# Source order for every engine and the transfer queue in the last stages of a hybrid decoder layer, with the attention cut into six phases

## The chip, the cores and the metric

The kernel runs on one core of a Trainium2 chip. The metric is the device time of one execution in microseconds (us). The engines are TensorE (PE in the rows), VectorE (DVE), ScalarE (ACT), GpSimd (POOL) and SyncE (SP), which issues nearly all transfers; each works through its own list of instructions in order and waits for semaphores of the others.

## What is computed

One decoder layer for 512 tokens of width 1024. The normalised input goes through one projection of 3,380 columns, cut into three mixers: gated linear attention (4 heads, chunks of 64), sparse attention (6 heads of 64; an indexer's scores pick the 128 keys of each query) and a causal pooling mixer (4 groups with windows 2, 4, 8, 16). Each is multiplied by a SiLU gate; one output projection, a residual and a final norm follow. Cut to the core:

```python
h = rmsnorm(x, norm_g[l])
p = jnp.einsum('btd,dc->btc', h, w_in[l])
(gq, gk, gv, gz, ggate, dq, dk, dv, dgate, qi, ki, wi, pu, pgate) = split_cols(p)
glog = log_sigmoid(einsum('btr,rc->btc', gz, gla_gate_w2[l]) + gla_gate_b[l]) / 16
y_gla = rmsnorm(gla_mixer(gq, gk, gv, glog), gla_norm_g[l]) * silu(ggate)
# dsa: score = sum over index heads of relu(qi.ki) * wi, causal; top 128 keys of a query;
#      softmax over them of q.k / 8 + bias[bucket(distance)]; times v
y_dsa = dsa_mixer(dq, dk, dv, qi, ki, wi, rel_bias) * silu(dgate)
y_pool = pool_mixer(pu, pool_w[l], pool_scale[l]) * silu(pgate)
x = x + einsum('btc,cd->btd', concat([y_gla, y_dsa, y_pool]), w_out[l])
return rmsnorm(x, final_norm_g)
```

## The kernel before

**Products.** Matmuls are done in parts: a weight or an operand is split into a high part (`hi_of`, ScalarE) and a low part (`lo_of`, VectorE, or POOL for the weight halves named in `POOL_LO`), and a product is three matmuls, high by high, high by low and low by high. A weight chunk (`qd`, `n1` to `n4`, `dg`, `pg`, `c2`, `c1`, `pu`, `c0`) comes in two halves through a few staging buffers; `halves("c11")` splits half 1 of chunk `c1`. The output weights `wo0` to `wo3` come through the same buffers in two loads each, and four pairs of `oh`, `ol` pieces are split from each.

**Order.** `open_run` starts the layer. Then `project` goes through the chunks; each chunk has steps (projections into one accumulator), and after half a step ("mid") or a whole one `hooks` runs what the table `after` names for that place. So the table puts the other work between the projections: index scores, the top-128 rounds (`topk(i, ...)`: one MAX8 and one MATCH_REPLACE8 over the query tile's row of 256, 384 or 512 columns take eight keys; 16 rounds each for tiles 1, 2, 3), the linear attention (`gla_...`), and from chunk `pu` on the sparse attention. Inside `manual_schedule` an engine's list is the order of the source for the engines named; others are filled by a scheduler. Up to chunk `c1` that names TensorE, ScalarE, VectorE and POOL; from the first attention item on, and in `finish`, only TensorE and POOL. SyncE's list is the scheduler's after the opening.

**Attention.** An item (i, g) is query tile i (128 queries) and head pair g. `att_l` makes bias and mask in L on POOL; `att_q` makes the scores (TensorE, ps from KK, KL and QQ), adds them to L and takes the row's extremum (VectorE, L694), the exponential (ScalarE, L696), the reciprocal (VectorE, L698) and the normalised L (POOL, L700); `att_t` transposes L (tpp) and copies it to pt (ScalarE for one head, VectorE for the other); `att_v` makes ov and yt, and their parts yDh and yDl. KK, KL and QQ hold keys and queries of a head pair; `take_dqk` makes them from a projection (qkr), its high part qkh and its low part qkl, which are put in place by transfers. Chunk `c1` brings the queries of pair 2 in its first step and keys in its second; the first scores, item (0,2), stand right behind it.

**Linear attention.** `gla_gates` multiplies GS by w2r (split in high and low at that place) to z, then `gtA` (ScalarE) and `gtM` (VectorE); `gla_sums` subtracts and scans; `gla_scores` makes AT with masked copies; `gla_out` (po) needs AT. `pool_branch` is four scans and small operations on VectorE. `finish` holds the output projection (op), the rest of the attention and the norm.

Of the kernel before, what the change touches and what calls it, by code (L numbers as in the profile page):

```python
# [29 lines left out]
POOL_LO = ("n11", "n21", "n31", "n41", "pg0", "c20", "c21", "c10", "pu0")  # L30
# [39 lines left out]
def hybrid_layer(  # L70
# [102 lines left out]
    def bias_load():  # L173
        with tc.issue_after(chunks[-1].load.ins):
            nc.sync.dma_start(TB, bias_tab.rearrange("p (h j) -> p h j", h=6))
# [182 lines left out]
    def take_dqk(c, j):  # L358
        for step, cc in enumerate((0, 1) if j == 1 else (1, 0)):
# [31 lines left out]
    def gla_gates():  # L391
# [5 lines left out]
        hi_of(w2r, w2s)  # L397
        lo_of(w2r[32:48], w2s[32:48], w2r[32:48])
# [176 lines left out]
    def pool_branch():  # L575
        pm = S("pm", [P, 2, T])
        for j in range(2):
            for b, w in ((0, (2, 8)[j]), (64, (4, 16)[j])):
                r = slice(b, b + 64)
                nc.vector.tensor_tensor_scan(pm[r, j, :], up[r, j, 16:528], up[r, j, 16 - w:528 - w], 0.0,  # L580
                                             op0=ALU.add, op1=ALU.subtract)
            pf = S("pf", [P, 16], bufs=2, name=f"pf{j}")
            nc.vector.tensor_tensor(pf, pm[:, j, 0:16], rcn[:, j, :], op=ALU.mult)
            nc.vector.scalar_tensor_tensor(pm[:, j, :], pm[:, j, :], rcw[:, j:j + 1], up[:, j, 16:528],
                                           op0=ALU.mult, op1=ALU.subtract)
            nc.vector.tensor_tensor(pm[:, j, 0:16], pf, up[:, j, 16:32], op=ALU.subtract)
# [24 lines left out]
    halves = lambda *names: [partial(half, n[:2], int(n[2])) for n in names]  # L611
    after = {
# [465 lines left out]
```

## Time and profile before

| | us |
|---|---|
| median of 3 runs (lowest to highest) | 281.83 (281.48 to 282.24) |
| the profiled execution, and its span | 280.79, 279.0 |
| TensorE busy (share of the span), instructions | 251.5 (90%), 1498 |
| VectorE | 203.4 (73%), 444 |
| ScalarE | 120.7 (43%), 251 |
| POOL | 95.3 (34%), 107 |
| mean granted clock of TensorE | 0.959 |

The profile's page gives the busy time of every engine over the span, and a strip of 40 slices. In the strip TensorE has eights and nines nearly everywhere, with one slice at 5 about three fifths through; the granted clock falls to 5 and 7 there. The waits and the timeline then tell what stood in the way, and the windows give busy time and clock of any stretch. A busy share is an average over stages: what counts for the end is which engine's next instruction is late.

### The profile page before, as it was taken

How to read it: one execution, taken by the hardware profiler on the slowest of the kernel's cores; microseconds unless marked ns; L12 is line 12 of the kernel's file. 1: busy time of each engine (PE TensorE's matmuls, PEld its weight loads, DVE VectorE, ACT ScalarE, POOL GpSimd, SP SyncE). 2: the span in 40 equal slices, each digit the busy share in tenths (PEclk: the TensorE clock that was granted, in tenths of full speed). 3: DMA queues.
4: the chain of work that ended last, by engine and by line, in shares of the span. 5: the costliest groups of instructions: out<-in, count | busy, mean ns of one | idle time of the engine just before them, and what ended most of it. 6: DMA issues, size and time to landing. Idle time of an engine off the chain costs nothing.

```text
span 279.0 us, 4219 instructions
## 1 busy us (share of the span) xinstructions
PE 251.5 (90%) x1498; PEld 210.6 (76%) x1498; DVE 203.4 (73%) x444; ACT 120.7 (43%) x251; POOL 95.3 (34%) x107
## 2 busy tenths in 40 slices
PE   8999999689999899999999519987995999999991
PEld 5788979589999798888888408765883677787890
DVE  3969688958999859896969788889597565345222
ACT  5737386574734263363123243333474354232111
POOL 1633464413093086135303005631244455100010
PEclk9999999979999999999999957999799899999998
DMA  7796402225213220315246832840383000023221
GB/s 256 275 318 276 157 15 82 79 75 188 78 49 105 76 66 12 93 60 152 76 109 179 252 87 62 209 162 0 78 301 75 0 4 0 0 89 130 84 78 75
DMA packets 11780, 31.09 MB, mean 111 GB/s; under 512 B 1600, under 2 KB 1600, under 8 KB 11760
## 3 DMA queue, kind: packets, MB, share of 16 engines
q1 hardware_dynamic: 11328, 30.05, 34.6%
q10 hardware_dynamic: 432, 0.79, 0.8%
q8 instruction: 12, 0.20, 0.3%
q14 instruction: 8, 0.07, 0.1%
HBM read 23.91 MB, written 2.10 MB: 93 GB/s over the span
## 4 chain that ended last, share of the span: by engine, by line
PE 57%; DVE 25%; ACT 6%; issue 4%; DMA 4%; POOL 1%; POOLq 0%; DVEq 0%; ACTq 0%
PE op L749 13%; PE pf L915 8%; DVE scs L457 5%; PE pn_n L197 5%; DMA wr_wo<-in_w_out 4%; DVE m L456 4%; PE ov L720 3%; PE tpp L709 2%; DVE pm L580 2%; PE ps L692 2%; PE warm L936 2%; DVE wl_c L99 2%; ACT L L696 2%; DVE ol L99 2%; DVE wl_n L99 1%
## 5 line engine op out<-in xcount | busy, mean ns | idle before, releaser
L700 POOL TENSOR_SCALAR L<-L,ast 128x128 f32<-128x128 f32 (+3 forms) x24 | 12.7, 540 | 56.0 <-DVE ast L698 50.0
L456 DVE MAX8 m<-scs 128x8 f32<-128x256 f32 (+2 forms) x48 | 26.5, 553 | 0.2
L457 DVE MATCH_REPLACE8 scs<-m,scs 128x256 f32<-128x256 f32 (+2 forms) x48 | 26.1, 543 | 0.0
L197 PE MATMUL pn_n<-wh_n,hTh 128*128 128x270 f32 (+1 forms) x128 | 22.1, 296 | 0.0
L197 PE MATMUL pn_n<-wl_n,hTh 128*128 128x270 f32 (+1 forms) x128 | 21.8, 294 | 0.0
L197 PE MATMUL pn_n<-wh_n,hTl 128*128 128x270 f32 (+1 forms) x128 | 21.6, 292 | 0.0
L696 ACT ACTIVATE L<-L,ast 128x128 f32<-128x128 f32 (+3 forms) x24 | 13.3, 556 | 18.7 <-DVE ast L694 18.7
L209 PE MATMUL pt_c<-hTh,wh_c 128*128 128x512 f32 x48 | 19.7, 410 | 0.0
L197 PEld LDWEIGHTS pn_n<-wh_n,hTh 128*128 128x128 f32 x128 | 18.7, 193 | 0.7 <-issue 0.4
L210 PE MATMUL pt_c<-hTl,wh_c 128*128 128x512 f32 x48 | 19.1, 399 | 0.0
L211 PE MATMUL pt_c<-hTh,wl_c 128*128 128x512 f32 x48 | 19.1, 399 | 0.0
L197 PEld LDWEIGHTS pn_n<-wl_n,hTh 128*128 128x128 f32 x128 | 18.7, 197 | 0.0
L197 PEld LDWEIGHTS pn_n<-wh_n,hTl 128*128 128x128 f32 x128 | 18.4, 193 | 0.0
L692 PE MATMUL ps<-KK,QQ 128*128 128x128 f32 (+3 forms) x24 | 8.8, 373 | 10.1 <-DMA QQ<-qkl 9.1
L96 ACT ACTIVATE oh<-wr_wo 128x512 fp32r<-128x512 f32 x16 | 9.0, 622 | 18.4 <-DMA wr_wo<-in_w_out 13.6
L754 DVE TENSOR_TENSOR xr<-op,xr 128x512 f32<-128x512 f32 (+1 forms) x8 | 5.3, 657 | 15.7 <-PE op L749 15.7
L755 ACT ACTIVATE sqo<-xr 128x512 f32<-128x512 f32 (+1 forms) x8 | 4.8, 605 | 25.4 <-DVE xr L754 25.4
L99 DVE TENSOR_TENSOR ol<-wr_wo,oh 128x512 fp32r<-128x512 f32 x16 | 11.4, 744 | 5.1 <-ACT oh L96 5.0
L909 POOL TENSOR_TENSOR acc<-acc,sqk 128x512 f32<-128x512 f32 x7 | 9.5, 1354 | 15.1 <-ACT sqk L907 15.1
L99 POOL TENSOR_TENSOR wl_n<-wr_n,wh_n 128x1080 fp32r<-128x1080 f32 (+1 forms) x4 | 10.1, 2513 | 12.3 <-ACT wh_n L96 10.3
L692 PEld LDWEIGHTS ps<-KK,QQ 128*128 128x128 f32 x24 | 4.8, 201 | 11.6 <-DMA QQ<-qkl 9.5
L670 POOL TENSOR_TENSOR L<-scs,TB 128x512 f32<-128x512 f32 x9 | 12.6, 1403 | 0.0
(241 smaller groups left out, 718.4 us busy)
## 6 DMA issues: line engine op xcount, KB each, us to landing
wr_wo<-in_w_out SPq DMA_DIRECT2D x8, 512.0 KB, 3.7
wr_c<-in_w_in SPq DMA_DIRECT2D x6, 512.0 KB, 3.4
wr_n<-in_w_in SPq DMA_DIRECT2D x4, 540.0 KB, 7.9
wr_n<-in_w_in SPq DMA_DIRECT2D x4, 536.0 KB, 3.5
xr<-in_x SPq DMA_DIRECT2D x4, 512.0 KB, 4.1
xk<-in_x_t SPq DMA_DIRECT2D x7, 256.0 KB, 5.2
wk<-in_w_in SPq DMA_DIRECT2D x6, 256.0 KB, 5.0
KK<-qkh SPq DMA_DIRECT2D x12, 128.0 KB, 2.3
```

What stands on the lines that cost most here:

```text
L99: return (eng or nc.vector).tensor_tensor(dst, src, hi.bitcast(F32), op=ALU.subtract)
L197: mm(ps[:, 0:n], a[:, k, ts_], w[:, k, :], start=(h + part + k == 0), stop=(h == 1 and part == 2 and k == 3))
L209: mm(ps[:, t0:T], c.hi[h][:, k, cs], hTh[h][:, k, t0:T], start=(h + k == 0), stop=False)
L210: mm(ps[:, t0:T], c.hi[h][:, k, cs], hTl[h][:, k, t0:T], start=False, stop=False)
L211: mm(ps[:, t0:T], c.lo[h][:, k, cs], hTh[h][:, k, t0:T], start=False, stop=(h == 1 and k == 3))
L456: nc.vector.max(out=m8, in_=msk[i])
L457: nc.vector.match_replace(out=msk[i], in_to_replace=m8, in_values=msk[i], imm_value=TAKEN)
L692: mm(pss[b][:, 0:n], QQ[2 * g + b][:, i0:i0 + P], K[2 * g + b][:, 0:n], start=(K is KK), stop=(K is KL))
L696: nc.scalar.activation(L[:, b, 0:n], L[:, b, 0:n], AF.Exp, bias=st[:, b:b + 1], scale=-1.0, accum_out=st[:, 2 + b:3 + b])
L700: nc.gpsimd.tensor_scalar(L[:, b, 0:n], L[:, b, 0:n], st[:, 4 + b:5 + b], 1.0, op0=ALU.mult, op1=ALU.mult)
L749: mm(outs[t][a][:, 0:e - a], lhs, rhs, start=(first and yi == 0 and rhs is wh and lhs is yh), stop=(last and yi == len(ys) - 1 and lhs is yl))
L915: mm(pns[t], a[:, t * P:(t + 1) * P], w, start=(k + part == 0), stop=(k == KT - 1 and part == 2))
```

## The change

1. One `manual_schedule` block for all chunks and `finish`, naming TensorE, ScalarE, VectorE, POOL and SyncE: the source's order holds for all of them and for the transfers.
2. An attention item becomes six phases: l, q, n (reciprocal and normalise), t, v and y (the low part yDl), each with its place in `after` or `finish`. There is a new place, "end", behind a query or key step's transfers.
3. The split of w2r moves from `gla_gates` to `later_tables`; the logarithm becomes `gla_logs`, behind the split of `n30`; several weight splits move, and `c11` and `c00` get their low parts on POOL.
4. The top-128 rounds are set out so that all are placed by the end of the query step of `c1`; before, `topk(16, 2, 3)` put what remained behind `c1`.
5. The splits of the output weights (`split_out(n, h)`, two pieces each call) go to five places from `pu` on and into `finish`; before they stood together in `c0`. Their loads start while `c1` runs; `final_g` and the residual's x come in `finish`.
6. `pool_branch(j)` in two halves, `pool_low` and `out_norm` apart.

```diff
-POOL_LO = ("n11", "n21", "n31", "n41", "pg0", "c20", "c21", "c10", "pu0")
+POOL_LO = ("n11", "n21", "n31", "n41", "pg0", "c20", "c21", "c10", "c11", "pu0", "c00")
@@ later_tables
         nc.vector.tensor_copy(cm, of("cm"))
+        hi_of(w2r, w2s)
+        lo_of(w2r[32:48], w2s[32:48], w2r[32:48])
@@ take_dqk
                             nc.sync.dma_start(dst[2 * g + b][r:r + 64].bitcast(F32),
                                               src[64 * b:64 * b + 64].bitcast(F32))
+            hooks(c.name, step, "end")
@@ gla_gates
-        hi_of(w2r, w2s)
-        lo_of(w2r[32:48], w2s[32:48], w2r[32:48])
...
+
+    def gla_logs():
+        gtA = lt["gates"][0]
         nc.scalar.activation(gtA, gtA, AF.Ln, bias=1.0)
@@ after
-        ("n1", 3, "mid"): [partial(topk, 1, 2)],
-        ("n1", 3): [*halves("n30"), partial(topk, 1, 1, 3)],
+        ("n1", 3, "mid"): [*halves("n30"), lambda: gla_logs(), partial(topk, 1, 2)],
+        ("n1", 3): [partial(topk, 1, 1, 3)],
...
-        ("c1", 0): [late_tiles, *halves("pu1"), partial(topk, 2, 2, 3)],
-        ("c1", 1): [partial(topk, 16, 2, 3), *halves("c00", "c01")],
...
+        ("c1", 0, "mid"): [*halves("pu1"), partial(topk, 1, 2, 3)],
+        ("c1", 0, "end"): [*halves("c00"), partial(topk, 1, 2, 3)],
+        ("c1", 1, "mid"): [partial(topk, 1, 2, 3)],
+        ("c1", 1): [lambda: nc.gpsimd.memset(up[:, :, 0:16], 0.0), *att("l02", "l12")],
+        ("c1", 1, "end"): [*halves("c01"), partial(topk, 16, 2, 3), *att("q02")],
+        ("pu", 0, "mid"): att("n02", "q12"),
...
+        ("pu", 1, "mid"): [*att("v02", "t12", "q22"), lambda: pool_branch(0)],
+        ("pu", 1): [*att("y02", "n22"), lambda: split_out(0, 0), *att("v12", "l32")],
+        ("c0", 0, "mid"): [*att("y12", "t22", "q32"), lambda: pool_branch(1)],
+        ("c0", 0): att("n32", "l01"),
+        ("c0", 0, "end"): [lambda: split_out(1, 0), lambda: load_next(), *att("v22")],
+        ("c0", 1, "mid"): att("y22", "t32", "q01", "l11"),
...
+        ("c0", 1, "end"): [*att("v32", "q11", "l21"), lambda: split_out(0, 1)],
@@ att_q, att_n: the reciprocal and the normalising become a phase of their own
+    def att_n(i, g):
+
+        n = (i + 1) * P
+        L, st = Ls[i, g], asts[i, g]
         nc.vector.reciprocal(st[:, 4:6], st[:, 2:4])
@@ finish
-        att_t(0, 1), att_q(2, 1)
+        do("y32", "t01", "n11", "q21", "l00")
+        split_out(1, 1)
         out_part(1, 0, T, "G", first=True)
-        att_v(0, 1), att_t(1, 1), att_q(0, 0)
+        do("v01", "t11", "n21", "q00", "l31")
+        split_out(2, 0)
+        load_next()
...
         pool_mix()
         out_part(2, 0, T, "G", first=True)
-        att_v(1, 1), att_t(2, 1), att_q(3, 1)
+        do("y01")
+        pool_low()
+        do("v11", "t21", "n00", "q31", "l10")
+        split_out(3, 0)
         out_part(0, 0, T, "P")
...
+        do("y21", "v00", "t31", "n10", "q20", "l30")
+        split_out(3, 1)
+        do("y00")
         out_part(2, 0, T, "P")
         out_part(0, 0, T, "D", last=True)
@@ the end of the kernel
-    with tc.manual_schedule(engines={ENG.PE, ENG.Activation, ENG.DVE, ENG.Pool}):
-        project(("qd", "n1", "n2", "n3", "n4", "dg", "pg", "c2", "c1"))
-    with tc.manual_schedule(engines={ENG.PE, ENG.Pool}):
-        att_q(0, 2)
-        project(("pu", "c0"))
+    with tc.manual_schedule(engines={ENG.PE, ENG.Activation, ENG.DVE, ENG.Pool, ENG.SP}):
+        project([name for name, _ in CHUNKS])
         finish()
```

What an engine's list holds in a row, at three places. First SyncE's transfers around the end of chunk `c1` (QQ_110 and QQ_111 are the queries of pair 2, KK and KL keys, wr_wo output weights in their staging buffers), before:

```order
L381 DMA KK_115<-qkh_1642 64x512 x2
L147 DMA wr_wo_1667<-in_w_out 128x1024
L375 DMA QQ_110<-qkh_1695 64x512
L375 DMA QQ_111<-qkh_1695 64x512
L381 DMA KL_120<-qkl_1643 64x512 x2
L147 DMA wr_wo_1801<-in_w_out 128x1024
L381 DMA KL_121<-qkl_1643 64x512 x2
L375 DMA QQ_110<-qkl_1696 64x512
L375 DMA QQ_111<-qkl_1696 64x512
L381 DMA KK_112<-qkh_1749 64x512 x2
```

and after:

```order
L382 DMA KK_115<-qkh_1668 64x512 x2
L382 DMA KL_120<-qkl_1669 64x512 x2
L382 DMA KL_121<-qkl_1669 64x512 x2
L147 DMA wr_wo_1686<-in_w_out 128x1024
L147 DMA wr_wo_1688<-in_w_out 128x1024
L376 DMA QQ_110<-qkh_1724 64x512
L376 DMA QQ_110<-qkl_1725 64x512
L376 DMA QQ_111<-qkh_1724 64x512
L376 DMA QQ_111<-qkl_1725 64x512
L382 DMA KK_112<-qkh_1763 64x512 x2
```

The low parts of QQ moved from behind an output-weight load and the keys to directly behind the high parts; two output-weight loads stand ahead of all four. Second, VectorE at the same place (m_2 and m_3 are rounds of tiles 2 and 3, their number last; L460 and L462 close a tile's selection), before, beginning right behind the qkr whose parts go to QQ:

```order
L99 TENSOR_TENSOR wl_pu_1702<-wr_pu_1452,wh_pu_1701 128x1024
L456 MAX m_2_14_1705<-scs 128x8
L457 MATCH_REPLACE scs<-m_2_14_1705,scs 128x384
L456 MAX m_3_11_1708<-scs 128x8
L457 MATCH_REPLACE scs<-m_3_11_1708,scs 128x512
L456 MAX m_2_15_1711<-scs 128x8
L457 MATCH_REPLACE scs<-m_2_15_1711,scs 128x384
L460 TENSOR_SCALAR scs<-scs 128x384
L456 MAX m_3_12_1715<-scs 128x8
L99 TENSOR_TENSOR ol_2099<-wr_wo_1801,oh_2098 128x2x256
L457 MATCH_REPLACE scs<-m_3_12_1715,scs 128x512
L99 TENSOR_TENSOR qkl_1696<-qkr_1694,qkh_1695 128x512
```

and after:

```order
L458 MAX m_3_14_1683<-scs 128x8
L459 MATCH_REPLACE scs<-m_3_14_1683,scs 128x512
L99 TENSOR_TENSOR wl_pu_1704<-wr_pu_1464,wh_pu_1703 128x1024
L458 MAX m_3_15_1707<-scs 128x8
L459 MATCH_REPLACE scs<-m_3_15_1707,scs 128x512
L462 TENSOR_SCALAR scs<-scs 128x512
L367 SCALAR_TENSOR_TENSOR qkr_1723<-pt_c_1690,rsb 128x512
L99 TENSOR_TENSOR qkl_1725<-qkr_1723,qkh_1724 128x512
L369 TENSOR_TENSOR qkr_1762<-pt_c_1737,rsb 128x512
```

All rounds moved ahead of the first qkr shown, and nothing stands between it and its qkl. Third, VectorE after the scores of item (2,2), in chunk `pu` (L694 and L708 are the addition of the scores, ast the row's statistics), before:

```order
L694 ISA L_1819,ast_1890<-ps_1891,L_1819 128x384
L694 ISA ast_1890 128x1
L694 ISA L_1819,ast_1890<-ps_1892,L_1819 128x384
L694 ISA ast_1890 128x1
L99 TENSOR_TENSOR yDl<-yt_1873,yDh 128x128
L387 TENSOR_TENSOR up<-pt_pu_1857,rsb 128x512
L698 RECIPROCAL ast_1890<-ast_1890 128x2
```

and after:

```order
L708 ISA L_1851,ast_1883<-ps_1885,L_1851 128x384
L708 ISA ast_1883 128x1
L582 SCALAR_TENSOR_TENSOR pm<-up 64x512 x2
L585 TENSOR_TENSOR pf_1897<-pm,tab 128x16
L586 SCALAR_TENSOR_TENSOR pm<-pm,tab,up 128x512
L588 TENSOR_TENSOR pm<-pf_1897,up 128x16
L388 TENSOR_TENSOR up<-pt_pu_1854,rsb 128x512
L99 TENSOR_TENSOR yDl<-yt_1870,yDh 128x128
L717 RECIPROCAL ast_1883<-ast_1883 128x2
```

One half of the pool branch, two scans and three small operations, moved between the scores and their reciprocal; the other half stands likewise behind the scores of (3,2), ahead of a qkr of `c0`.

## Rows read from the trace of the kernel before

**Rows 1.** TensorE's waits, the whole span: line, what it waited for, us, times, longest.
```profile
PE ps L692 <- DMA QQ<-qkl: 9.1, 1, 9.1
PE z L401 <- DVE w2r L99: 3.5, 1, 3.5
PE tpp L709 <- POOL L L700: 2.4, 1, 2.4
```

**Rows 2.** Busy time by stretches: length, engines' us (instructions), granted clock, DMA.
```profile
98.00:153.60 55.60, 55.60 (x343) 46.96 (x339) 45.50 (x113) 20.47 (x37) 23.49 (x16) 1.00 0.33 94
160.80:171.05 10.25, 4.49 (x12) 3.66 (x13) 8.19 (x22) 5.31 (x9) 1.17 (x4) 0.50 0.39 89
167.70:272.80 105.10, 98.89 (x541) 77.89 (x541) 65.70 (x155) 38.67 (x107) 34.64 (x45) 0.95 0.27 84
194.90:198.30 3.40, 3.40 (x15) 2.91 (x13) 2.92 (x5) 1.42 (x3) 2.04 (x3) 0.50 0.34 77
```

**Rows 3.** TensorE's timeline: start, us, line, operation, [idle before <-releaser].
```profile
95.50 0.46 PE L528 MATMUL po<-gv,AT 128*128 128x96 f32 x2 [1.13 <-ACT AT L515]
...
156.71 0.39 PE L210 MATMUL pt_c<-hTl,wh_c 128*128 128x512 f32 x1
156.94 0.40 PE L211 MATMUL pt_c<-hTh,wl_c 128*128 128x512 f32 x1
166.42 0.47 PE L692 MATMUL ps<-KK,QQ 128*128 128x128 f32 x1 [9.08 <-DMA QQ<-qkl]
...
194.10 1.05 PE L720 MATMUL ov<-pt,dv 128*64 128x128 f32 x12 [1.90 <-ACT pt L711]
...
272.51 0.28 PE L749 MATMUL op<-oh,yDl 128*128 128x256 f32 x1
```

**Rows 4.** SyncE's queue of transfers, timeline, 154 to 165 us.
```profile
154.32 1.11 SPq L375 DMA_DIRECT2D QQ<-qkh  x2
...
156.81 0.54 SPq L147 DMA_DIRECT2D wr_wo<-in_w_out  x1
...
164.21 1.10 SPq L375 DMA_DIRECT2D QQ<-qkl  x2
```

**Rows 5.** VectorE's timeline, from 52 to 190 us.
```profile
57.99 1.41 DVE L403 TENSOR_SCALAR gtM<-z,tab 128x512 f32<-128x512 f32 x2 [1.30 <-ACT gtA L402]
...
63.72 1.27 DVE L99 TENSOR_TENSOR wl_n<-wr_n,wh_n 128x1072 fp32r<-128x1072 f32 x1 [2.34 <-ACT wh_n L96]
...
67.17 2.89 DVE L412 TENSOR_TENSOR gtM<-gtM,gtA 128x512 f32<-128x512 f32 x1
...
151.09 1.95 DVE L99 TENSOR_TENSOR qkl<-qkr,qkh 128x512 fp32r<-128x512 f32 x1
152.96 0.68 DVE L366 SCALAR_TENSOR_TENSOR qkr<-pt_c,rsb 128x512 f32<-128x512 f32 x1
...
162.23 0.69 DVE L99 TENSOR_TENSOR ol<-wr_wo,oh 128x512 fp32r<-128x512 f32 x1 [1.03 <-ACT oh L96]
...
163.50 0.68 DVE L99 TENSOR_TENSOR qkl<-qkr,qkh 128x512 fp32r<-128x512 f32 x1
...
188.85 2.44 DVE L580 TENSOR_TENSOR_SCAN pm<-up 64x512 f32<-64x512 f32 x2
```

**Rows 6.** ScalarE's timeline, 154 to 162 us.
```profile
154.21 1.04 ACT L96 ACTIVATE wh_pu<-wr_pu 128x1024 fp32r<-128x1024 f32 x1
161.57 0.63 ACT L96 ACTIVATE oh<-wr_wo 128x512 fp32r<-128x512 f32 x1 [6.32 <-DMA wr_wo<-in_w_out]
```

**Rows 7.** Groups by line and shape, VectorE: busy us, mean ns, idle before.
```profile
L456 DVE MAX8 m<-scs 128x8 f32<-128x512 f32 x16 | 11.0, 686 | 0.0
L457 DVE MATCH_REPLACE8 scs<-m,scs 128x512 f32<-128x512 f32 x16 | 10.8, 676 | 0.0
```

**Rows 8.** DMA issues: count, KB of one, median us from issue to landing.
```profile
QQ<-qkl SPq DMA_DIRECT2D x6, 128.0 KB, 2.4
```

**Rows 9.** POOL's timeline near 150 us.
```profile
150.07 2.41 POOL L99 TENSOR_TENSOR wl_pu<-wr_pu,wh_pu 128x1024 fp32r<-128x1024 f32 x1 [14.76 <-ACT wh_pu L96]
```

More of the change, by code (lines that the diff above doesn't have):

```diff
@@ L173, in bias_load @@
     def bias_load():
-        with tc.issue_after(chunks[-1].load.ins):
-            nc.sync.dma_start(TB, bias_tab.rearrange("p (h j) -> p h j", h=6))
+        nc.sync.dma_start(TB, bias_tab.rearrange("p (h j) -> p h j", h=6))
     def bias_table():
@@ L573, in hybrid_layer, with pool_branch @@
     pool = {}
[L575 to L586, printed above, removed]
-        pool["pm"] = pm
+    def pool_branch(j):
+        pm = pool.setdefault("pm", None) or S("pm", [P, 2, T])
+        pool["pm"] = pm
+        for b, w in ((0, (2, 8)[j]), (64, (4, 16)[j])):
+            r = slice(b, b + 64)
+            nc.vector.tensor_tensor_scan(pm[r, j, :], up[r, j, 16:528], up[r, j, 16 - w:528 - w], 0.0,
+                                         op0=ALU.add, op1=ALU.subtract)
+        pf = S("pf", [P, 16], bufs=2, name=f"pf{j}")
+        nc.vector.tensor_tensor(pf, pm[:, j, 0:16], rcn[:, j, :], op=ALU.mult)
+        nc.vector.scalar_tensor_tensor(pm[:, j, :], pm[:, j, :], rcw[:, j:j + 1], up[:, j, 16:528],
+                                       op0=ALU.mult, op1=ALU.subtract)
+        nc.vector.tensor_tensor(pm[:, j, 0:16], pf, up[:, j, 16:32], op=ALU.subtract)
     def pool_mix():
@@ L595, in pool_mix, with pool_low @@
             hi_of(yPh[:, j, :], pg[:, j, :])
+    def pool_low():
+        for j in range(2):
             lo_of(yPl[:, j, :], pg[:, j, :], yPh[:, j, :])
@@ L611, in hybrid_layer, with phase @@
     halves = lambda *names: [partial(half, n[:2], int(n[2])) for n in names]
+    def phase(n):
+        {"l": att_l, "q": att_q, "n": att_n, "t": att_t, "v": att_v, "y": att_y}[n[0]](int(n[1]), int(n[2]))
+    att = lambda *names: [partial(phase, n) for n in names]
     after = {
@@ L731, in out_open @@
         xr = S("xr", [P, D], bufs=2, name=f"xr{t}")
[L732 to L733 removed]
+        nc.sync.dma_start(xr, x2[t * P:(t + 1) * P, :])
         outs[t].update(xr=xr, sq=S("sqx", [P, D], name=f"sqo{t}", bufs=1), fs=S("fs", [P, 5], bufs=2, name=f"fs{t}"))
@@ new lines, in out_last @@
+        out_part(t, E, D, "GPD", first=True, last=True)
+        residual(t, 0, T, 0)
+        residual(t, T, E, 1)
+        nc.gpsimd.tensor_tensor(xf[:, 0:T], xr[:, 0:T], fg[:, 0:T], op=ALU.mult)
+        nc.vector.tensor_scalar(fs[:, 3:4], fs[:, 0:1], fs[:, 1:2], EPS, op0=ALU.add, op1=ALU.add)
+        nc.vector.tensor_tensor(xf[:, T:E], xr[:, T:E], fg[:, T:E], op=ALU.mult)
+        nc.vector.tensor_tensor(xr[:, E:D], outs[t][E][:, 0:D - E], xr[:, E:D], op=ALU.add)
+        nc.vector.scalar_tensor_tensor(sq[:, E:D], xr[:, E:D], 1.0 / 1024.0, xr[:, E:D],
+                                       op0=ALU.mult, op1=ALU.mult, accum_out=fs[:, 2:3])
@@ L811, in finish @@
+        residual(1, 0, T, 0)
+        out_norm(0)
+        do("y20")
+        out_part(1, T, D, "GPD", first=True, last=True)
         out_close(0)
-        out_part(1, 0, T, "D", last=True)
-        residual(1, 0, T, 0)
-        att_v(2, 0), att_t(3, 0)
-        out_part(1, T, D, "GPD", first=True, last=True)
+        out_open(2), out_open(3)
+        do("v30")
         residual(1, T, D, 1)
-        out_close(1)
-        out_open(2), out_open(3)
-        att_v(3, 0)
+        do("y30")
         out_part(2, 0, T, "D", last=True)
+        out_norm(1)
@@ L847, in out_tiles, with split_out @@
         return [S(f"o{hl}{half}{q}", [P, 2, T], F32R) for hl in "hl"]
-    def split_out(n):
-        part, j = divmod(n - n_in, 2)
+    def split_out(n, h):
+        part, j = divmod(n, 2)
         cs = slice(256 * j, 256 * j + 256)
-        for q in range(4):
+        for q in (2 * h, 2 * h + 1):
             if j == 0:
```

124 lines of the change are left out of this document (56 added, 68 removed).

## The prediction

> **What bounds the kernel now.** I read first how long TensorE waits and for whom, then its clock by stretches, then its own timeline to place both, and last the queue of transfers and the VectorE rows that its two long waits point to. TensorE works nearly all the time: the list of its waits [rows 1] has one wait of 9.1 us for the query operand QQ, one of 3.5 for w2r, one of 2.4 for POOL's normalised L, and [rows 3] show one of 1.90 for a pt copy; the others are about one or less. A wait costs twice. In [rows 2] the granted clock is 0.50, which is 1.2 GHz, from 160.80 to 171.05 behind the QQ wait, and again for 3.4 us behind the wait of 1.90 at 194.10; two more such stretches, alike, follow the waits for w2r and for L. At half speed 3.4 us do the work of 1.7, so I charge 1.7 us for each. The reader should see in [rows 2] also that TensorE is busy for 98.89 of the 105.1 us between 167.70 and 272.80, where the last matmul ends (272.51 + 0.28, [rows 3]): what stands behind the QQ wait is dense. From 272.8 to the span's end at 279.0 lie 6.2 us of tail, which the change leaves as it was.
>
> **The QQ wait, the main term.** The last projection matmul before it ends at 156.94 + 0.40 = 157.3, the scores start at 166.42 [rows 3] and the next projection step at 167.70, where the third window of [rows 2] begins. In [rows 4] the hi parts of QQ go out at 154.32, but the lo parts at 164.21, behind an output-weight load (156.81) and four key transfers. The lo part could not be made earlier: VectorE finished qkr at 153.6, then made wl_pu and top-128 rounds, stood still 1.03 us for the split of an output weight that itself waited 6.32 us on ScalarE for its load, and made qkl at 163.50 [rows 5, 6]. In the changed order qkl follows qkr at once, both behind the last round, and the four QQ transfers follow them with only the two output-weight loads ahead.
>
> Does VectorE have room to finish the rounds that early? Two of 384 and five of 512 columns stand behind qkr in the old order. A round of 512 is 0.686 + 0.676 = 1.36 us [rows 7]; with 384 taken in proportion (1.02), seven are 8.9, and about 0.8 for the closing selections gives 9.7. Three rounds (about 3) are moved ahead of 95.5 as well, so 6.7 remain to be placed where VectorE idles 55.60 - 45.50 = 10.1 us between 98.00 and 153.60 [rows 2]. They fit. The chain then is qkr 0.68, the hi part on ScalarE 0.63 (the time of its shape in [rows 6]), qkl 0.68 and four issues of about 0.55 (1.11 for two [rows 4]), the last landing 2.4 us later [rows 8]: 0.68 + 0.63 + 0.68 + 1.65 + 2.4 = 6.0 from the end of the projection step that feeds it. The next step, which TensorE runs meanwhile, is 24 matmuls at 0.23 us, the spacing in [rows 3], or 5.5. So 0.5 us are left at the least; I take 0.1 for overlap of issue and landing, with 0 to 2 as bounds (2: qkl stretched as at 151.09, below, by 1.27). Gone with the wait is half speed in the scores (1.28 us between 166.42 and 167.70, about 0.5 at full speed) and in the projection step after them.
>
> POOL gets the low parts of c11 and c00, one instruction of 2.4 us each, as its wl_pu [rows 9], and VectorE loses both. What such a neighbour costs is seen at 151.09: qkl took 1.95 us beside POOL's wl_pu, against 0.68 for the same shape at 163.50, 1.27 lost. If both hit VectorE on TensorE's path they cost 2.5, if neither does nothing. I take nothing, since ScalarE makes the hi part of a half, 1.04 us [rows 6], between qkh and POOL's start, and qkl is done by then. The Trainium skill, "SBUF — State Buffer", section "SBUF: two separate sides", calls the port pair of the two engines an exclusive lock that the later one waits for during the whole instruction, which speaks against this part of the change; by it two hits would cost up to 4.8 us and the time would be 275.3, where the measured row gives 273.0.
>
> **The w2r wait.** The split of w2r moves to an earlier hook, so the 3.5 us and the 1.7 of half clock behind them go at that place. But TensorE then comes to the output of the first linear-attention tile at 95.50 - 1.13 - 3.54 - 1.7 = 89.1, and its AT is only there at 95.5 [rows 3], at the end of a VectorE chain. That chain loses two idles, 1.30 at gtM and 2.34 at wl_n [rows 5], and 0.41 of w2r; it gains two rounds that were behind AT before (about 1.1 and 0.9): 2.1 us earlier. The first gtM subtraction took 2.89, beside POOL, where a qkr of its shape took 0.68 [rows 5]; if that goes it is 4.3 earlier. I take 2.8, so the wait here grows to 3.6, and since waits of 1.9 to 3.5 were each followed by a stretch at half clock I charge 1.7: the gain at the end of c1 is 2.8 - 1.7 = 1.1, rounded to 1.0, bounds 0.4 and 4.3.
>
> **The last stage.** By now TensorE reaches the scores at 156.3 and the pu projection at 156.4 + 0.5 = 156.9. What follows is 105.1 less 6.2 of idle time (105.1 - 98.89) less three half-clock charges (5.1; the first of them is the piece from 167.70 to 171.05): 93.8. With 6.2 of tail the span would be 256.9. To this come new waits, because the order of VectorE and ScalarE is now fixed where the scheduler had filled in:
> - In the c0 stage the reciprocal of item (2,2) and later the first qkr of c0 stand behind the four scan pieces of one pool branch; two scans alone are 2.44 us [rows 5]. The chain from qkr to QQ's landing is 6.0 as above; TensorE's cover is half a step (2.8) and one product of about 1.0 (the 12 matmuls of ov at 194.10 took 1.05 [rows 3]): 2.2 of wait, 4.7 if the scans come first. I take 3.5 and 1.7 of half clock; bounds 0 and 6.4.
> - In the finish ten of the sixteen output-weight splits, 0.63 on ScalarE [rows 6] and 0.69 on VectorE [rows 5] each, now lie between exponentials, norms and copies. In two places TensorE needs what stands right behind such a pair: the pool projection behind yt of (0,1), the D part of the first output behind yDl of (0,0). A pair delays by 2 x 0.63 + 0.69 = 1.95, or 2.0; I take one for each place, 3.8 in all with a little cover, and 1.7 of half clock once: 5.5, bounds 0 and 12.
>
> The rest costs nothing that I can see: later tables, the split of the attention into phases and the memset add no instruction; of loads moved behind others, the last four output weights have the finish as cover. Span 256.9 + 5.2 + 5.5 = 267.6. The profiled execution had 280.79 for a span of 279.0, 1.8 outside, and lay 1.0 under the median of 281.83: 267.6 + 1.8 + 1.0 = 270.4, I say **270.5 us**.
>
> **Rivals.**
> - Dense: neither stage makes new waits. For it: TensorE had none for 30 us at the end of before, and phases are spread a full step apart. 270.5 - 10.7 = 259.8; with a remnant up to 264.
> - The splits bite: all five pairs in the finish cost their 2.0, not two, and a second half-clock stretch comes: 270.5 + 6.2 + 1.7 = 278.4.
> - Slower: a wait at every phase of the finish. The prices are in [rows 1, 3]: 2.4 for POOL's normalising and 1.9 for a pt copy, with 1.7 at half clock behind each: about 3.85. The gain of 11.3 and the 5.5 already charged pay for 4.4 of them, so it decides from five of the finish's dozen blocks on; with six the time is 288. Against it: the same phases stood in the same engines before and two of them waited. The Trainium skill's page "TensorE: Matmul & The Clock Gate", section "HAM oscillation — how this bites in real kernels", tells of kernels whose every tile waits and so starts at the lower clock; by that rule this case would recur, and the trace agrees as far as the waits of 1.90, 2.4 and 3.5 go.
> - The change does not do what it says: QQ still lands late, since the two weight loads ahead of it wait for POOL's low parts to free their buffers, and the rounds do not fit. If 9.1 of wait with its half clock stays, 280 to 282.
>
> **How the numbers follow.** Forecast 266 to 274: 0.50. Dense: 0.25. Splits bite: 0.12. QQ late: 0.07. Slower: 0.06. The range from 260 to 279 leaves out the slower case, most of QQ late, some of the splits case and the lowest end of dense, together under 0.2. A measurement of this kernel tells about 0.3% (0.8 us) from no change: faster takes the first three cases and a part of QQ late, 0.92; same 0.02; slower 0.06.
>
> **What would show it.** In the waits of TensorE w2r should be absent, QQ at most 2 us before the first scores, and AT at po near 3.5 us. The scores of (0,2) start near 156.4, pu near 157. QQ lo leaves SyncE before 156. A wait at tpp of (3,2) or the scores of (0,1) shows the c0 term, one at pp or yDl the finish term. Wrong would be the sum if TensorE stops before pu for more than 3 us, if the clock is at 0.50 in more than four stretches after pu, or if the last matmul ends later than 268.

## The result: 283.5 us, 0.8% slower

The changed kernel takes 283.53 us in the median of 20 runs (282.13 to 285.67); the kernel before took 281.49 in 20 runs beside it. The ratio is 1.0082, with a 95% interval of 1.0058 to 1.0107. The forecast was 270.5 in 260 to 279: wrong in sign and outside its range. The profiled execution is the longest of the 20, 285.67 for a span of 283.2, so it lies 2.1 us above the median; a part of that may be the clock, told below.

TensorE's waits in the changed kernel, whole span (line, what it waited for, us, times, longest):

```profile
PE ps L706 <- DMA QQ<-qkl: 6.8, 4, 5.1
PE op L770 <- DVE yDl L99: 4.0, 1, 4.0
PE po L530 <- ACT AT L517: 3.2, 2, 3.0
PE tpp L728 <- POOL L L719: 2.3, 4, 1.0
PE pp L594 <- DVE yt L742: 1.9, 1, 1.9
```

Against [rows 1] the wait for w2r is gone and the one for QQ has shrunk from 9.1 to 5.1, but the one for AT has grown from 1.13 ([rows 3]) to 2.97, and those for yDl and yt are new. TensorE's timeline places them:

```profile
91.81 0.46 PE L530 MATMUL po<-gv,AT 128*128 128x96 f32 x2 [2.97 <-ACT AT L517]
...
161.72 0.45 PE L706 MATMUL ps<-KK,QQ 128*128 128x128 f32 x1 [5.12 <-DMA QQ<-qkl]
...
163.10 0.73 PE L208 MATMUL pt_pu<-hTh,wh_pu 128*128 128x512 f32 x1
...
235.82 0.49 PE L770 MATMUL op<-oh,yDl 128*128 128x512 f32 x1 [4.02 <-DVE yDl L99]
...
276.73 0.28 PE L770 MATMUL op<-oh,yDl 128*128 128x256 f32 x1
```

The pu projection starts at 163.10, 4.6 us before its old place (167.70), so the change did shorten the way there. The last matmul ends at 277.0, 4.2 after its old place (272.8, [rows 3]). All that was gained ahead of pu, and 4.2 us more, is lost behind it: 113.9 us there instead of 105.1. Windows over these stretches (length, busy us of the engines, granted clock, DMA):

```profile
92.80:99.70 6.90, 6.90 (x57) 6.40 (x57) 6.14 (x16) 5.35 (x11) 4.43 (x5) 0.53 0.26 90
161.40:168.30 6.90, 6.32 (x16) 5.06 (x17) 0.76 (x5) 0.99 (x4) 1.51 (x3) 0.51 0.76 194
195.70:202.60 6.90, 6.10 (x17) 4.36 (x18) 1.67 (x7) 0.99 (x4) 0.40 (x1) 0.52 0.50 165
163.10:277.01 113.91, 103.49 (x541) 79.61 (x541) 60.42 (x149) 38.54 (x108) 34.59 (x44) 0.92 0.24 79
```

Behind pu TensorE idles 113.91 - 103.49 = 10.4 us, where the third window of [rows 2] had 6.2. Its clock is at half speed (1.2 GHz) in stretches of 6.9 us behind AT, behind QQ and in the c0 stage, twice as long as that of [rows 2] at 194.90 (behind QQ [rows 2] had 10.25); two more of 3.4 follow the waits for yt and yDl.

### The profile page after: what moved, and what is told of

Same layout as the page of the kernel before. It is cut to its first block, busy times and chain, and to the rows that moved or that the text cites. A ratio compares the mean times of both kernels' runs of the same rounds, so it can differ in the third digit from the quotient of the medians.

```text
span 283.2 us, 4207 instructions
## 1 busy us (share of the span) xinstructions
PE 256.6 (91%) x1498; PEld 212.6 (75%) x1498; DVE 198.8 (70%) x442; ACT 120.3 (42%) x251; POOL 101.3 (36%) x109
## 4 chain that ended last, share of the span: by engine, by line
PE 44%; DVE 28%; issue 13%; ACT 5%; DMA 4%; POOL 3%; SPq 0%; POOLq 0%; ACTq 0%; DVEq 0%
PE op L770 10%; DVE scs L459 5%; PE pf L960 4%; DVE m L458 4%; DVE ol L99 3%; PE pn_n L196 3%; DMA QQ<-qkl 3%; ACT L L710 3%; PE pt_c L208 2%; PE pt_c L209 2%; PE pt_c L210 2%; DVE scs L444 2%; DMA wk<-in_w_in 2%; POOL L L719 1%; PE pt_dg L208 1%
## 5 line engine op out<-in xcount | busy, mean ns | idle before, releaser
L719 POOL TENSOR_SCALAR L<-L,ast 128x128 f32<-128x128 f32 (+3 forms) x24 | 14.4, 612 | 53.7 <-DVE ast L717 45.0
L99 DVE TENSOR_TENSOR ol<-wr_wo,oh 128x512 fp32r<-128x512 f32 x16 | 14.2, 929 | 8.3 <-ACT oh L96 8.3
L210 PE MATMUL pt_c<-hTh,wl_c 128*128 128x512 f32 x48 | 19.8, 413 | 0.0
L209 PE MATMUL pt_c<-hTl,wh_c 128*128 128x512 f32 x48 | 19.8, 413 | 0.0
L99 POOL TENSOR_TENSOR wl_c<-wr_c,wh_c 128x1024 fp32r<-128x1024 f32 x5 | 11.9, 2389 | 14.8 <-PE pt_c L210 10.2
L708 DVE CUSTOM_DVE_ANT_0 L<-ps,L 128x128 f32<-128x128 f32 (+3 forms) x24 | 10.8, 482 | 8.4 <-PE ps L706 7.2
L96 ACT ACTIVATE yDh<-yt 128x128 fp32r<-128x128 f32 x12 | 3.7, 310 | 28.4 <-DVE yt L742 28.4
L954 POOL TENSOR_TENSOR acc<-acc,sqk 128x512 f32<-128x512 f32 x7 | 10.7, 1533 | 10.7 <-ACT sqk L952 10.6
L770 PE MATMUL op<-oh,yDl 128*128 128x512 f32 (+1 forms) x27 | 10.0, 371 | 4.0 <-DVE yDl L99 4.0
L96 ACT ACTIVATE qkh<-qkr 128x512 fp32r<-128x512 f32 x6 | 3.8, 632 | 23.2 <-DVE qkr L369 9.9
```

The source lines that it names most:

```text
L99: return (eng or nc.vector).tensor_tensor(dst, src, hi.bitcast(F32), op=ALU.subtract)
L209: mm(ps[:, t0:T], c.hi[h][:, k, cs], hTl[h][:, k, t0:T], start=False, stop=False)
L210: mm(ps[:, t0:T], c.lo[h][:, k, cs], hTh[h][:, k, t0:T], start=False, stop=(h == 1 and k == 3))
L719: nc.gpsimd.tensor_scalar(L[:, b, 0:n], L[:, b, 0:n], st[:, 4 + b:5 + b], 1.0, op0=ALU.mult, op1=ALU.mult)
L770: mm(outs[t][a][:, 0:e - a], lhs, rhs, start=(first and yi == 0 and rhs is wh and lhs is yh), stop=(last and yi == len(ys) - 1 and lhs is yl))
```

## The experiments

Times are medians; the kernel before ran beside each set at 280.9 to 281.5, and each ratio is to it. "Less" and "more" are against the changed kernel's 283.5, which was not run again beside the sets; reckoned by the ratios they come out up to 0.7 us different.

### The wait in the finish

**e1.** yDl of (0,0) ahead of the split:

```diff
-        do("y21", "v00", "t31", "n10", "q20", "l30")
+        do("y21", "v00", "t31", "y00", "n10", "q20", "l30")
         split_out(3, 1)
-        do("y00")
```

> Edit: in the finish the phase y of item (0,0) (its low part yDl) stands ahead of the scores of (2,0) and of the split of output weights (3,1), otherwise as the changed kernel. Theory: TensorE's wait of 4.02 us for yDl at the D part of the first output, and the 1.7 us at half clock behind it, come only from that split (two oh on ScalarE, behind two exponentials, and two ol on VectorE), so both go and the time falls by 5.7 from 283.5 to about 277.8, ratio to the kernel before near 0.987. Rival: the chain of (2,0) or the POOL normalising behind it is late by nearly as much, so the wait moves to the next transposes and the time falls by at most 1.5.

279.38, ratio 0.9938 (0.9906 to 0.997): 4.1 less. In the changed kernel VectorE had made yt long before its low part:

```profile
230.13 0.28 DVE L742 TENSOR_TENSOR yt<-ov,dg 128x128 f32<-128x128 f32 x1
...
233.44 2.14 DVE L99 TENSOR_TENSOR ol<-wr_wo,oh 128x512 fp32r<-128x512 f32 x2 [1.42 <-ACT oh L96]
235.50 0.28 DVE L99 TENSOR_TENSOR yDl<-yt,yDh 128x128 fp32r<-128x128 f32 x1
```

yt ends at 230.4 and its low part, 0.28 us of work, comes at 235.50, behind a pair of output-weight pieces that first waited for ScalarE. With y00 moved, the wait for yDl is gone; 1.4 us of wait are left one output later, for the next yt, that of (3,1), which VectorE now makes at 234.12 behind the same pair. No half clock follows: 4.0 - 1.4 + 1.7 = 4.3, about as measured. The cause is shown; the forecast of 5.7 had missed that the pair delays this yt as well, so a part of the rival came too.

### The wait for QQ, in layers

SyncE's queue in the changed kernel (start, time for the issue, transfers):

```profile
151.12 2.88 SPq L382 DMA_DIRECT2D KL<-qkl  x4
154.10 1.03 SPq L147 DMA_DIRECT2D wr_wo<-in_w_out  x2
155.23 0.47 SPq L376 DMA_DIRECT2D QQ<-qkh  x1
155.78 0.55 SPq L376 DMA_DIRECT2D QQ<-qkl  x1
```

The first scores need the first pair, whose lo part goes out at 155.78; they start at 161.72, 5.9 us later. The trace's own line on the twelve QQ transfers (from issue to landing) has the same:

```profile
DMA to landing us min/median/max: 2.2/2.4/5.8
```

Just ahead in the queue stands 1 MB of output weights. And VectorE made qkr late, behind the last round:

```profile
152.57 0.68 DVE L459 MATCH_REPLACE8 scs<-m,scs 128x512 f32<-128x512 f32 x1
153.28 0.43 DVE L462 TENSOR_SCALAR scs<-scs 128x512 f32<-128x512 f32 x1
153.63 0.68 DVE L367 SCALAR_TENSOR_TENSOR qkr<-pt_c,rsb 128x512 f32<-128x512 f32 x1
155.06 0.69 DVE L99 TENSOR_TENSOR qkl<-qkr,qkh 128x512 fp32r<-128x512 f32 x1 [0.75 <-ACT qkh L96]
```

The projection that feeds qkr ended some 5.5 us, one step, before c1's end at 156.6, at 151.1.

**e2.** The weight loads behind QQ:

```diff
-            if n < n_in - 1:
+            if n < n_in - 1 and name != "c1":
                 load_next()
...
-        ("c1", 0, "end"): [*halves("c00"), partial(topk, 1, 2, 3)],
+        ("c1", 0, "end"): [lambda: load_next(), *halves("c00"), partial(topk, 1, 2, 3)],
```

> Edit: the two loads of the first output weights are issued behind the four QQ transfers of pair 2 instead of ahead of them. Theory (the transfers wait in the DMA engines behind 1 MB of weights): the last QQ part, which was issued at 157.02 and landed at 161.7, 4.7 us later, lands in about 2.4, so the first scores start near 159 and the time falls by 2 to 3, to about 281. Rival (issue is the limit): SyncE's queue and VectorE set the moment, landing stays over 4 us, the wait stays at 5.1 and so does the time.

279.13, ratio 0.9937 (0.9905 to 0.997): 4.4 less. Queue and scores in e2:

```profile
155.62 0.46 SPq L376 DMA_DIRECT2D QQ<-qkl  x1
...
157.97 0.30 PE L706 MATMUL ps<-KK,QQ 128*128 128x128 f32 x1 [1.52 <-DMA QQ<-qkl]
...
159.27 0.30 PE L706 MATMUL ps<-KK,QQ 128*128 128x128 f32 x1 [0.88 <-DMA QQ<-qkl]
```

The lo part goes out only 0.16 sooner, yet the scores start 2.35 us behind it instead of 5.9. The waits for the two pairs fall from 5.12 and 0.27 to 1.52 and 0.88, and no half clock follows, which is why more was gained than forecast. The landing behind the weights was the largest layer: 4.4 of the 6.7 us that e4 gains below.

**e3.** Also the keys of pair 1 behind QQ (the eight transfers are kept in a list and sent after QQ; qkh and qkl get a third buffer).

> Edit: as e2, and the eight transfers of the keys of pair 1 are issued behind QQ as well. Theory (three layers: data, queue, landing): in the changed kernel SyncE is busy with those keys until 154.0 and with the weights until 155.1, while qkh is there at 155.0 and qkl at 155.7, so with the rounds still ahead of qkr the keys in the queue hide behind the data, and this run is like e2 within 0.5 us. Rival (the queue is the limit): QQ goes out 1 to 2 us sooner than in e2 and the wait shrinks by as much.

280.27, ratio 0.9958 (0.9927 to 0.9989), not to be told from e2; the wait is 1.53. The queue was not the limit while the data were late.

**e4.** Also the last round behind qkl:

```diff
-        ("c1", 0, "mid"): [*halves("pu1"), partial(topk, 1, 2, 3)],
+        ("c1", 0, "mid"): [*halves("pu1")],
```

> Edit: as e3, and the last top-128 round of tile 3 with its closing selection stands behind qkl instead of ahead of qkr. Theory: qkr no longer waits 1.9 us behind them, all three layers are gone, the wait at the first scores falls to about 1 us (from 5.1), the scores start near 157.5 and the time is about 4 to 5 below 283.5, near 279. Rival (what is gained ahead of the scores is lost behind them): the scores start as early, and the end moves by less than half of that.

276.82, ratio 0.9846 (0.9792 to 0.9901): 6.7 less, more than forecast. qkr is at 151.42, the last QQ out at 154.73, the scores start at 156.08 without a wait at their first matmul, and pu at 157.46. The theory holds for the weights and the rounds. What the keys count for once the rounds are gone was not run by itself: in the changed kernel they hold SyncE until 154.0, and e4 sends its first QQ at 152.85.

**e9.** The first scores half a step later, behind 12 matmuls of pu (`q02` moves from ("c1", 1, "end") to ("pu", 0, "mid")).

> Edit: the changed kernel with the scores of the first item (0,2) half a projection step later, in the middle of the first step of pu instead of ahead of it. It is also the control for the next run, whose TensorE order is the same. Theory: half a step (12 matmuls at 0.23, 2.8 us) hides that much of the 5.1 us of wait for QQ; the rest of about 2.3 stays, and the 3.4 us at half clock behind it fall to 1.7 or none: 4 to 5 less than 283.5, 279. Rival: the exponentials of (0,2) come later by as much and the transposes of (0,2) wait instead: less than 1 us.

279.48, ratio 0.9937 (0.991 to 0.9963): 4.0 less. The wait is 2.13. Half a step of cover is as good as moving the weights.

**e11.** The low parts of c11 and c00 back on VectorE:

```diff
-POOL_LO = ("n11", "n21", "n31", "n41", "pg0", "c20", "c21", "c10", "c11", "pu0", "c00")
+POOL_LO = ("n11", "n21", "n31", "n41", "pg0", "c20", "c21", "c10", "pu0")
```

> Edit: the changed kernel with the low parts of c11 and c00 back on VectorE. Theory: POOL's 2.4 us instructions cost VectorE little at these places, while 2 x 1.2 us more on VectorE put the last rounds and qkr later by up to 2.4 (c11's) and the first scores with them: 1 to 3 slower than 283.5. Rival (an operand port held by POOL during its whole instruction): VectorE loses up to 2 x 1.3 as qkl did beside wl_pu, so without them the time is the same or 1 to 2 faster.

287.48, ratio 1.0229 (1.019 to 1.0269): 4.0 more. The wait for QQ grows to 8.32, of which 1.35 is TensorE coming sooner in this execution; qkr comes 1.2 later (154.83), the scores start 1.85 later (163.57), and the half clock around them lasts 10.2 us for 6.8. So this part of the change was a gain, larger than I thought, because VectorE sets when QQ comes.

### The written order behind pu

**e6.** The split (1,1) behind the scores of (0,0):

```diff
-        split_out(1, 1)
         out_part(1, 0, T, "G", first=True)
         do("v01", "t11", "n21", "q00", "l31")
+        split_out(1, 1)
```

> Edit: the changed kernel with the output-weight split (1,1) behind the scores of (0,0) instead of ahead of the product of (0,1). Theory: the pool projection's wait of 1.91 for yt of (0,1) and the half clock behind it (1.7) come from that pair, so the time falls by 3.6, to about 280. Rival: two pairs now stand together ahead of the pool projection's results on VectorE, and the wait moves to the next product: less than 1 us.

283.02, ratio 1.0044 (0.9992 to 1.0097): no gain that can be told. The wait at the pool projection went, and that for yDl fell to 2.42, but 1.28 for pg came and the one for a pt copy grew from 0.77 to 1.63. The rival holds; its profiled execution took 279.54, 3.5 under the median, so the profile says little of the time.

**e7.** The second half of the pool branch one step later (from ("c0", 0, "mid") to ("c0", 1, "mid"), behind `l11`).

> Edit: the changed kernel with the second half of the pool branch one step later on VectorE, behind the scores of (0,1), where VectorE idles for 4.9 us. Theory: the reciprocal of (3,2) and the first qkr of c0 no longer stand behind its four operations (3.6 us), so the waits at the transposes of (3,2) (0.62 and 0.96) and at the scores of (0,1) (0.60 and 0.80) go, and with them the 3.4 us at half clock behind them: 6.4 in all, to about 277. Rival: POOL is the limit there (normalising (3,2) took 2.31 and its bias comes late), the waits stay within half, and at most 2 us are gained.

279.39, ratio 0.9957 (0.9919 to 0.9995): 4.1 less. Of the four waits one of 0.82 stays, and no half clock follows there (the changed kernel had a stretch of 6.8 us). The cause is right; two thirds of the size came.

**e10.** VectorE and ScalarE filled by the scheduler from pu on, with TensorE's list that of e9:

```diff
+    names = [name for name, _ in CHUNKS]
     with tc.manual_schedule(engines={ENG.PE, ENG.Activation, ENG.DVE, ENG.Pool, ENG.SP}):
-        project([name for name, _ in CHUNKS])
+        project(names[:-2])
+    with tc.manual_schedule(engines={ENG.PE, ENG.Pool, ENG.SP}):
+        project(names[-2:])
         finish()
```

> Edit: the changed kernel, but from chunk pu on VectorE and ScalarE are again filled by the scheduler as in the kernel before (TensorE, POOL and SyncE keep the source's order; TensorE's list is that of e9, and one output-weight load goes out behind the first QQ instead of later). Theory: the loss behind pu comes from the written order of VectorE and ScalarE (splits and the pool branch ahead of what TensorE waits for); the scheduler puts yDl of (0,0) and yt of (0,1) ahead of splits, so the waits of 4.0 and 1.9 and their half clock go and the time is 6 to 8 under e9, near 272. Rival: the phases, not the order, cost it: the same as e9 within 1.5.

272.29, ratio 0.9677 (0.9637 to 0.9717): 7.2 less than e9. All waits of TensorE above 0.3 us in it, but for the start:

```profile
PE ps L706 <- DMA QQ<-qkl: 6.7, 3, 4.3
PE po L530 <- ACT AT L517: 3.3, 2, 3.1
...
PE ps L706 <- DVE ast L708: 0.6, 1, 0.6
PE ov L739 <- DVE pt L730: 0.4, 1, 0.4
PE ps L706 <- DVE pt L730: 0.3, 1, 0.3
```

The waits for yDl, yt and POOL's L are gone although POOL's list is the same. So what the change lost behind pu is the written order of VectorE and ScalarE, not the phases. In one thing more it differs from e9, and this works against it: three output-weight loads, not two, go out ahead of QQ, and its wait there is 4.33 where e9 has 2.13.

### The w2r wait and AT

**e12.** The kernel before with the w2r split alone moved (the two lines from `gla_gates` to `later_tables`).

> Edit: the kernel before with one part of the change alone, the split of w2r in the earlier hook. Theory: the wait of 3.5 at z and its half clock go, but AT of tile 0 is hardly earlier, so a wait at po takes their place and the end moves by 0 to 1 us (ratio 0.996 to 1.000). Rival: the whole 5.2 is gained (ratio 0.982).

275.4, ratio 0.9808 (0.9773 to 0.9843). The rival holds: the whole 5.6 us. AT came as much sooner as TensorE did; VectorE on AT, first in e12, then in the changed kernel:

```profile
88.82 0.28 DVE L513 COPY_PREDICATED AT<-cm,pa 64x128 f32<-64x128 uint8 x1
```

```profile
90.81 0.28 DVE L515 COPY_PREDICATED AT<-cm,pa 64x128 f32<-64x128 uint8 x1
```

The difference, 2.0 us, is two top-128 rounds that the changed order has ahead of AT (25 there, 23 before). TensorE arrives at 88.7 in e12 and 88.8 in the changed kernel; the wait is 1.13 in one, 2.97 and 3.4 of half clock in the other.

**e5.** po one step later, in the changed kernel (`gla_out(0)` and `gla_scores(1)` from ("n4", 1) to ("n4", 2)).

> Edit: the changed kernel with the output of the first linear-attention tile (po) and the scores of the second one projection step later, so that AT is ready when TensorE comes. Theory: the gain at w2r (z starts 4.0 us earlier than in the kernel before) is only lost again at AT, in a wait of 2.97 and 3.4 us at half clock behind it; without that wait both are gained: the time falls by about 6 from 283.5, to 277 or 278. Rival: the next consumer of the same VectorE chain (tile 1 of the linear attention, the norm, the gate weights) is late instead and the time falls by less than 2.

282.21, ratio 1.0033 (0.9994 to 1.0071): 1.3 less. AT is no longer waited for; instead a projection waits 2.39 for ScalarE's dv, with 1.7 at half clock, and the wait at the first scores grows to 6.16. The rival holds.

**e13.** The two rounds behind AT:

```diff
-        ("n3", 2): [turn_kd, partial(topk, 1, 1, 2)],
-        ("n3", 3, "mid"): [*halves("dg0"), partial(topk, 1, 1)],
+        ("n3", 2): [turn_kd, partial(topk, 1, 1)],
+        ("n3", 3, "mid"): halves("dg0"),
...
-        ("n4", 0): [bias_table, partial(topk, 1, 1, 2, 3)],
+        ("n4", 0): [bias_table, partial(topk, 1, 1, 2, 3), partial(topk, 1, 1, 2)],
```

> Edit: the changed kernel with two top-128 rounds (the eighth of tile 2, the thirteenth of tile 1) behind AT of the first linear-attention tile instead of ahead of it, as they stood in the kernel before. Theory: AT is 2.0 us sooner, its wait falls from 2.97 to about 1.1 and brings no half clock (before: 1.7 to 3.4), so TensorE runs 4 to 5 us ahead at the end of the linear attention; but the last round and QQ are no sooner, so the wait for QQ grows by nearly as much and the time falls by 0 to 2 from 283.5. Rival: the gain is kept to the end: 4 to 5.

278.94, ratio 0.9942 (0.9912 to 0.9972): 4.6 less. The wait at po is 0.99, and that for QQ stays at 4.91 rather than growing: VectorE's chain to QQ moved with TensorE, since in the changed kernel it had been waiting for it (2.02 for a pU, 1.19 for dg's projection). My theory of a fixed limit there fell; the gain is kept.

**e14.** e4 with the two rounds behind AT.

> Edit: e4 (QQ ahead of the weights and of the keys of pair 1, the last round behind qkl) with the two rounds behind AT as in e13. Theory: with QQ no longer late the gain at AT is kept: 3.5 to 5 less than e4's 276.8, 272 to 273. Rival: VectorE, with two rounds more behind AT, is late for qkr by as much: the same as e4 within 1.

275.17, ratio 0.9787 (0.9724 to 0.9849): 1.6 less than e4, between the theory (3.5 to 5) and the rival (within 1). In the profiles pu starts 3.8 sooner than in e4 (153.69 for 157.46) and the last matmul ends 2.9 sooner; behind pu TensorE idles 2.7 us more than in e4, the largest new wait being 1.66 for xr. How much is kept in the median is open: the intervals of e4 and e14 overlap.

### All together

**e8.** e4 with e1, e5, e6 and e7.

> Edit: the changed kernel with the transfers of QQ ahead of the weights and of the keys of pair 1, the last round behind qkl, yDl of (0,0) ahead of its split, and the three edits of the other runs of this set. Theory (waits and their half clock add up and nothing else moves): the changed kernel had 20.9 us of waits for other engines and 13.7 of half clock in a span of 283.2; of these some 3 and 2 stay, so the time is near 255 to 258. Rival (each wait taken away uncovers one behind it): 265 to 272.

265.79, ratio 0.9441 (0.9379 to 0.9504). Half clock remains in two stretches, and the waits that e5 and e6 had uncovered are all there (2.4, 1.6 and 1.3). The rival, "each wait taken away uncovers one behind it", gave the better figure.

**e16.** The edits of e4, e1, e6, e7, e9 and e13.

> Edit: e14 with yDl of (0,0) ahead of its split, the split (1,1) behind the scores of (0,0), the second pool half a step later, and the first scores half a step later. Theory (waits and half clock add up): e8 (265.8) had 2.4 + 1.7 at the projection behind the late po and 0.7 for QQ, which go here: 261 to 262, with few waits over 1.5 and one or two stretches at half clock left. Rival: VectorE's rounds behind AT come back as a wait at the first scores: as e8, 265 to 267.

263.2, ratio 0.9363 (0.9313 to 0.9413): 20 us less than the changed kernel and 6.4% less than the kernel before, the fastest here, between the theory (261 to 262) and the rival (265 to 267). The waits above 1 us that are left, but for the start:

```profile
PE ov L748 <- ACT pt L739: 1.8, 2, 1.6
PE ps L715 <- DVE pg L604: 1.3, 1, 1.3
PE po L539 <- ACT AT L526: 1.2, 2, 1.0
```

## Why the prediction was wrong, point by point

The sum was built of work, waits and half clock, against a span. Each part can be set beside the profiled execution:

| | forecast | measured | miss |
|---|---|---|---|
| pu starts | 156.9 | 163.1 | 6.2 |
| waits behind pu | 7.3 | 10.4 | 3.1 |
| half clock behind pu | 3.4 | 9.0 | 5.6 |
| the work itself | 93.8 | 94.5 | 0.7 |
| tail | 6.2 | 6.2 | 0 |
| span | 267.6 | 283.2 | 15.6 |

The half clock is 2.6 for the rest of the stretch behind QQ, 3.0 in the c0 stage and 1.7 twice in the finish. The profiled execution is the longest of the 20; against the median the miss is 13.0.

- **The frame held.** The work behind pu, found by taking idle time and half clock out of the old trace, is right to 0.7 us.
- **The QQ wait: the failed step.** "They fit": the rounds were to fit VectorE's idle time before 153.6, so that qkr follows its projection at once. The total did fit, the place did not: the last round and its closing selection stood in front of qkr, which came at 153.63 instead of 151.1. And the landing was taken at the median of 2.4, "with only the two output-weight loads ahead"; those loads made it 5.8. The bounds of 0 to 2 had left out both; their upper end priced only a stretched qkl. In [rows 4] the old lo parts went out 6.9 us behind the last load (164.21 for 156.81 + 0.54), so the median of [rows 8] does not show what a load directly ahead does. The old trace did hold a sign of it: the high parts at 154.32, 1.6 us behind a load issued at 152.72, landed in 3.0 to 3.2 us. e2 and e4 show both causes. Of the 6.2 us, 5.0 are this wait, 0.9 the scores at half clock (with a wait of 0.27 for the second pair), 0.3 the term below. With the 2.6 of half clock that the same wait leaves behind pu, this step makes 8.5 of the 15.6.
- **The w2r term.** The gain at c1's end was 0.7 for a forecast of 1.0, right in size, and the two added rounds were in the working. What was not seen is how much hangs on them: e12 gains 5.6 without them, e13 gains 4.6 in the changed kernel. AT came 3.7 sooner than before (forecast 2.8), but 3.4 of half clock followed where 1.7 was charged.
- **The c0 stage.** Waits of 0.51, 0.62, 0.96, 0.60 and 0.80 make 3.5, as forecast; for the last four the reason given is shown (e7), the first was not tested. The half clock cost 3.0, not 1.7.
- **The finish.** The two places named, yt of (0,1) and yDl of (0,0), are where it waited. The first cost 1.9, as priced; the second 4.0 instead of 1.9. Both pairs stand behind two exponentials of ScalarE, and VectorE idles 1.42 for each. But at the second its ol took 2.14 for two instead of 1.29, and TensorE stopped 0.2 us before VectorE was done with the scores ahead of the pair (231.8 for 232.0), at the first 1.0 us behind that (210.7 for 209.65). With 0.97 of smaller waits it is 6.9 for 3.8.
- **Half clock, the most mis-sized term.** "I charge 1.7 us for each" came from three alike stretches. It failed in two ways: three of the places were followed by 6.9 us, twice as much, and the finish, where the sum charged one stretch for two waits, had two. Why the stretch is twice as long at some places stays open.
- **The cheap parts.** Low parts on POOL were put at nothing; e11 shows them worth 4.0. The reason I gave for no contention held for QQ's qkl, but the next qkl, at 158.02, did meet c00's low part:

```profile
158.02 1.71 DVE L99 TENSOR_TENSOR qkl<-qkr,qkh 128x512 fp32r<-128x512 f32 x1 [0.70 <-ACT qkh L96]
```

```profile
156.84 2.35 POOL L99 TENSOR_TENSOR wl_c<-wr_c,wh_c 128x1024 fp32r<-128x1024 f32 x1 [10.17 <-PE pt_c L210]
```

It lost 1.0 us, off TensorE's path. VectorE ended 0.54 after POOL here, and 0.56 after it in the pair of [rows 5] and [rows 9]. That agrees with the Trainium skill, "SBUF — State Buffer", section "SBUF: two separate sides": the later one is blocked for the whole instruction of the first. In these two rows, then, the cost (1.0 and 1.27 us) depends on when the later one comes and is no fixed price.
- **The signs.** Of the three that were to show the sum wrong two came: TensorE stopped 5.12 us before pu, and the last matmul ended at 277.0, behind 268. Half clock came in four stretches after pu, not in more. That QQ lo leaves SyncE before 156 came true (155.78), and it landed late all the same.
- **The rivals.** What happened is none of the four as written. "Slower" had the sign, but not the cause: TensorE did not wait at every phase of the finish. "QQ still lands late" was right in place but priced at 280 to 282 with nothing behind it, and "the splits bite" was right in part behind pu: the second half-clock stretch in the finish came, but two pairs made TensorE wait, not five. They were kept as alternatives, each with its own chance, and what was right in each came together. Since they have different causes, the case of both belonged in the list, at about 281 + (278.4 - 270.5) = 289 by my own prices.

## What to carry to other kernels

When an order is written out by hand, look at each small operation that another engine waits for (here a low part of 0.28 us, a reciprocal, a copy) and at what stands right ahead of it, on its own engine and on the one that feeds it; such places make most of the 8.8 us lost behind pu, where the change had brought 4.6 ahead of it. A free total ("the rounds fit") says nothing of the place: ask of every instruction on the late chain what the new order puts directly in front. And a transfer that someone waits for must go out ahead of the large loads, not behind them.

## What the runs showed of the hardware

**The clock behind one and the same wait differs between executions.** The wait at po is 2.97 us in the changed kernel and in e7. In the window of 6.9 us behind it the granted clock is 0.53 in the first (shown above) and 0.75 in e7:

```profile
92.80:99.70 6.90, 6.90 (x67) 6.47 (x68) 5.96 (x16) 5.53 (x11) 4.25 (x5) 0.75 0.29 97
```

That is 3.4 us lost in one execution and 1.7 in the other, with the same instructions in the same place (e7's edit comes later). A wait of 0.99 at po was followed by 1.7 us in e13 and by none in e14. So a part of the spread of a kernel's times (3.5 us for the changed one) may be the clock alone; that it is the whole of it was not shown. The four executions of e14 go that way: 274.1 and 274.2 at a mean granted clock of 0.985 and 0.979, 276.2 twice at 0.968. The Trainium skill, "TensorE: Matmul & The Clock Gate", section "Part 1: The HAM clock gate (the "warmup" mystery)", says that the gate's watch over TensorE runs freely and that the number of matmuls at the lower clock at a kernel's start varies from run to run; the two windows above show the like in the middle of a kernel.

**A small transfer right behind 1 MB of loads.** A part of QQ, 128 KB, took 5.8 us from issue to landing with two loads of 512 KB issued in the 1.7 us before it, and at most 2.4 in e2, where the same loads went out behind it:

```profile
DMA to landing us min/median/max: 2.2/2.3/2.4
```

The time goes with the number of loads ahead: 3.0 to 3.2 behind one (the kernel before, at 154.32), 5.5 to 5.8 behind two (the changed kernel), 7.3 to 7.5 behind three (e10, at 153.78).
